# Moving GpSimd's part of a decoder layer's middle stage to VectorE and ScalarE

## The chip, the cores and the metric

One core of a Trainium2 chip runs the whole kernel. The metric is the time of one execution on the device in microseconds; lower is better. Engines are named as in the profile: PE (matrix products, PEld its weight loads), DVE (VectorE), ACT (ScalarE), POOL (GpSimd), SP (which issues most transfers). Each engine carries out its own queue strictly in order; the order of every queue is fixed when the kernel is built, by a scheduler that plans with its own idea of durations.

## The reference

One layer for 256 new prompt tokens and 8 decoded tokens (264 columns, T), width 2048, all in fp32: a half-step SwiGLU FFN of width 5504, a mixing stage, a second FFN, a final norm. In the mixing stage half the width is windowed attention, the other half is RWKV-7 time mixing. What the change touches is the time mixing:

```python
prev = jnp.concatenate([shift0[:, None].astype(proj.dtype), proj[:, :-1]], axis=1)
xm = (proj + mu * (prev - proj)).astype(f32)          # token shift
...
a = jax.nn.sigmoid(a0.astype(f32) + al @ a2.astype(f32))
kk = k * k_k.astype(f32)
k = k * (1.0 + (a - 1.0) * k_a.astype(f32))
...
kk = kk / jnp.maximum(jnp.sqrt(jnp.sum(kk * kk, axis=-1, keepdims=True)), 1e-12)
...
def step(S, inp):
    r_t, lw_t, k_t, v_t, kk_t, a_t = inp
    sa = jnp.einsum('bhij,bhj->bhi', S, -kk_t)
    S = (S * jnp.exp(lw_t)[:, :, None, :] + sa[..., None] * (kk_t * a_t)[:, :, None, :]
         + v_t[..., None] * k_t[:, :, None, :])
    return S, jnp.einsum('bhij,bhj->bhi', S, r_t)
```

## The kernel before

**Activations** lie transposed: 128 features on the partitions, 264 tokens along the free dimension. A **weight block** of 128 x 512 goes through `chunk` (lines 115 to 124): SP loads it into `raw` (ring of 6), ACT casts it to `hi` (ring of 4, line 122), and `lo = raw - hi` is made by DVE or, in the mixing stage for the third of a tile's four blocks (`LOP = (8,)`, argument `pool`), by POOL. Three products of 128 x 128 by 264 columns per 128 rows (hi by hi, hi by lo, lo by hi) give fp32 accuracy; a full tile is 16 x 3 = 48 products into one of three PSUM tiles `acc`.

**The stages.** First FFN, mixing, second FFN. In the FFNs PE works on such tiles only. In **mixing** 38 tiles of the input projection come in the order of `SEQ`: two tiles for the decay and gate inputs (`la`, `sgl`), then for each of 8 head pairs p three tiles (receptance, key, value: `xrr`, `xk`, `xv`) in four batches of two pairs, then keys and values of attention (4), then queries (8). Then the output projection in three passes (`PASS`).

**Side work.** After every weight block `gemm` calls `tick`, which advances every open generator by one step, so that small work is laid between blocks; the scheduler then orders it further by priority.

- `shifted` (331 to 341): DVE evicts a tile times the norm's factor into `pj` (columns 1 to 264; column 0 is zeroed by POOL for each tile); POOL subtracts neighbours, for the 256 prompt columns and the 8 decode columns; DVE's `scalar_tensor_tensor` multiplies by mu and adds.
- `prep` (351 to 451), one per pair: decay and gate factors, normalised key `kk`, products `b = kk*a` and `rk`, the factors `W`, `Wi`; then the key blocks. `KR` holds -kk and r times their decay, `BK` holds b and kx divided by decay, per chunk c of 64 tokens two slots of 64 columns: the head on partitions 0 to 63 has b in slot 0 and kx in slot 1, the other head the reverse, so that four half-height POOL products fill it. Line 420 multiplies both slots by `KR`; lines 443 to 450 transpose `BK` on PE and copy it to `t`.
- `chain` (463 to 612), one per batch, after both preps: triangular systems by 30 scan steps on DVE (tiles `X`, `Xt`, `st`), to and from DRAM for the layout (`sa`, `sb`, `TT`), then a transposition (`TN`) and small products on PE, then the states and a group norm.
- `dec_rwkv`: the decode tokens' state update, 16 rounds of DVE and POOL products (`ld`, `XR`), once the last prep is done; `attend` and `dec_attend`: attention.

Temporaries come from a ring of `NT` = 27 tiles `t`, side PSUM from five tiles `m`.

Of the kernel before, what the change touches and what calls it, by code (L numbers as in the profile page):

```python
# [13 lines left out]
P = 128  # L14
# [12 lines left out]
BATCH = [2, 2, 2, 2]  # L27
CH, NRAW, NHL = 4, 6, 4
NACC, NM = 3, 5
NS, NH, NT, NLD = 53, 40, 27, 6  # L30
NGM, NKR, NUV, NTT = 10, 5, 3, 2
NSTEP = 4
DWAIT = (8, 8, 8, 4)
LOP = (8,)
PW = (2, 1, 3, 2, 2)
ALPHA = math.exp(-0.5)
LKV = 26
# [9 lines left out]
def body(tc, I, O):  # L47
# [46 lines left out]
    with ExitStack() as ctx:  # L94
# [28 lines left out]
                tt(e, lo[:, :w], raw[:, :w], hi[:, :w].bitcast(F32), ALU.subtract)  # L123
            return hi, lo

        def gemm(ps, src, xs, step=None, rng=None, pool=False, ahead=True):
            n = len(xs)
            for k0 in range(0, n, CH):
                k1 = min(n, k0 + CH)
                if rng and k0 not in rng:  # L130
                    continue
                hi, lo = chunk(src[:, k0 * P:k1 * P], k1 - k0, G if pool and k0 in LOP else V, ahead)
                for k in range(k0, k1):
                    xh, xl = xs[k]
                    c = slice((k - k0) * P, (k - k0 + 1) * P)
                    mm(ps[:, :T], hi[:, c], xh, k == 0, False)
                    mm(ps[:, :T], hi[:, c], xl, False, False)
                    mm(ps[:, :T], lo[:, c], xh, False, k == n - 1)
                if step:
                    step()  # L140
# [149 lines left out]
        def mixing_body(mx, n2, n3):  # L290
# [18 lines left out]
            tw = fix((65, T), "tw")  # L309
            G.memset(tw[64:65, :], 1.0)  # L310
            rs = fix((P, T), "rs")
            qd = fix((P, 2, NB, 4), "qd")
            XR = fix((P, 6, 64), "XR")
            yr = fix((P, 64), "yr")
# [7 lines left out]

            def win(t):
                ps = acc()
                gemm(ps, I["win"][t], n2.xs, tick, pool=True)
                if not have[0]:
                    n2.rstd(rs)
                    have[0] = True
                return ps

            def shifted(t, d):
                ps = win(t)
                pj = ring((P, 268), "pj", 3)
                G.memset(pj[:, 0:1], 0.0)
                with tc.high_priority():
                    tt(V, pj[:, 1:1 + T], ps[:, :T], rs, ALU.mult)
                G.tensor_copy(shc[:, t, :], pj[:, NP:NP + NB + 1])
                tt(G, d[:, :NP], pj[:, 0:NP], pj[:, 1:NP + 1], ALU.subtract)
                tt(G, d[:, NP:], ss[:, t, :], pj[:, NP + 1:NP + 1 + NB], ALU.subtract)
                stt(d, d, vc(VMU + t), pj[:, 1:1 + T], ALU.mult, ALU.add)  # L340
                return d

            la, sgl = fix((P, T), "la"), fix((P, T), "sgl")
# [7 lines left out]
            def prep(p, bt, k, xrr, xk, xv):  # L351
                lw = load(I["lw"][p], (P, 256))
                zp = mp()
                for tb in range(2):
                    mm(zp[:, tb * P:(tb + 1) * P], tw[0:65, tb * P:(tb + 1) * P], lw[0:65, 0:P])
                mm(zp[:, 256:264], lw[0:65, 0:P], tw[0:65, NP:T])
                ap = mp()
                mm(ap[:, :T], lw[64:128, P:2 * P], la[64:128, :])
                sg, a = tmp(), tmp()
                act(sg, zp[:, :T], AF.Sigmoid)  # L360
                act(a, ap[:, :T], AF.Sigmoid, bias=vc(VA0 + p))
                kk, sq = tmp(), tmp()
                act(kk, xk, AF.Copy, scale=vc(VKK + p))
                act(sq, kk, AF.Square)
                bor = tmp((P, P))
                ts(G, bor, bo, vc(VRK + p), ALU.mult)
                yield from pause(PW[0])
                nps = mp()
                mm(nps[:, :T], bo, sq)
                cps = mp()  # L370
                for tb in range(2):
                    mm(cps[:, tb * P:(tb + 1) * P], sg[:, tb * P:(tb + 1) * P], tri)
                nr = tmp()
                act(nr, nps[:, :T], AF.Sqrt)
                V.reciprocal(nr, nr)
                cv = cps[:, :NP].rearrange("p (c t) -> p c t", c=4)
                W, Wi = tmp((P, 4, 65)), tmp((P, 4, 64))
                G.memset(W[:, :, 0:1], 1.0)
                act(W[:, :, 1:65], cv, AF.Exp, scale=-ALPHA)
                act(Wi, cv, AF.Exp, scale=ALPHA)  # L380
                tc.keep_in_program_order(act(XD[:, 1, p, :], sg[:, NP:T], AF.Exp, scale=-ALPHA))
                G.tensor_copy(wc[:, p, :], W[:, :, 64])
                yield from pause(PW[1])
                b, kx, rk = tmp(), tmp(), tmp()
                stt(kk, nr, 1e12, kk, ALU.min, ALU.mult)
                tt(G, b, kk, a, ALU.mult)
                ts(V, a, a, 1.0, ALU.subtract, vc(VKA + p), ALU.mult)
                stt(kx, a, 1.0, xk, ALU.add, ALU.mult)
                tt(G, rk, xrr, kx, ALU.mult)
                yield  # L390
                BK, KR = ring((P, 4, 2, 64), "bk", 2), ring((P, 3, 4, 64), "kr", NKR)
                bt.KR[k] = KR
                stt(KR[:, 0], c4(kk), -1.0, W[:, :, 0:64], ALU.mult, ALU.mult)
                tt(G, KR[:, 1], c4(xrr), W[:, :, 1:65], ALU.mult)
                for h in range(2):
                    r = HALF[h]
                    tt(G, BK[r, :, h, :], c4(b)[r], Wi[r], ALU.mult)
                    tt(G, BK[r, :, 1 - h, :], c4(kx)[r], Wi[r], ALU.mult)
                for i, src in ((0, kk), (2, b), (3, xv), (4, kx), (5, xrr)):
                    G.tensor_copy(XD[:, i, p, :], src[:, NP:T])  # L400
                vp = mp()
                for tb in range(2):
                    TE.transpose(vp[:, tb * P:(tb + 1) * P], xv[:, tb * P:(tb + 1) * P], ident)
                for e in range(2):
                    for h in range(2):
                        A.copy(bt.UV[HALF[1 - h], e:4:2, k, HALF[h]],
                               vp[HALF[e], :256].rearrange("p (c t) -> p c t", c=2)[:, :, HALF[h]])
                yield from pause(PW[2])
                bps = mp()
                mm(bps[:, :T], bor, rk)  # L410
                bv = tmp()
                bt.bv[k] = bv
                tt(V, bv, bps[:, :T], xv, ALU.mult)
                G.tensor_copy(bvdec[:, p, :], bv[:, NP:T])
                yield
                for h in range(2):
                    r = HALF[h]
                    gp = mp()
                    for c in range(4):
                        mm(gp[:, c * P:(c + 1) * P], BK[r, c, :, :], KR[r, 0:2, c, :])  # L420
                    gm = ring((P, 4, P), "gm", NGM)
                    bt.Gm[k][h] = gm
                    tt(V, gm, gp.rearrange("p (c t) -> p c t", c=4), bc(msk.unsqueeze(1), (P, 4, P)), ALU.mult)
                    for blk in range(2):
                        x = blk * 32
                        SP.dma_start(
                            scr[bt.i].rearrange("(h b k c) (s t) -> h b k s c t", h=2, b=2, c=4, s=32)[h, blk, k],
                            gm[h * 64 + x:h * 64 + x + 32, :, x:x + 32])
                    yield
                kp = mp()  # L430
                for tb in range(2):
                    TE.transpose(kp[:, tb * P:(tb + 1) * P], KR[:, 0, 2 * tb:2 * tb + 2, :], ident)
                for e in range(2):
                    for h in range(2):
                        A.copy(KR[HALF[h], 0, e:4:2, :],
                               kp[HALF[e], :256].rearrange("p (c t) -> p c t", c=2)[:, :, HALF[h]])
                gv = mp()
                for h in range(2):
                    r, o = HALF[h], HALF[1 - h]
                    for c in range(4):  # L440
                        mm(gv[r, c * 64:c * 64 + 64], bt.Gm[k][h][o, c, 0:64], bt.UV[o, c, k, r])
                A.copy(KR[:, 2], gv[:, :256].rearrange("p (c t) -> p c t", c=4))
                for tb in range(2):
                    bp = mp()
                    for j in range(2):
                        TE.transpose(bp[:, j * P:(j + 1) * P], BK[:, 2 * tb + j, :, :], ident)
                    t = tmp((P, 2, P))
                    A.copy(t, bp[:, :256].rearrange("p (c t) -> p c t", c=2))
                    bt.BT[k].append(t)
                    yield  # L450
                bt.left -= 1
# [560 lines left out]
```

## Time and profile before

| | us |
|---|---|
| median of 3 runs | 2128.84 (2128.02 to 2131.24) |
| the profiled execution | 2127.34 |
| its span, first to last instruction | 2125.2 |
| first input-projection tile evicted | 778.2 |
| last input-projection tile evicted | 1207.4 |
| first output-projection tile evicted | 1250.1 |
| last output-projection tile evicted | 1357.2 |

The profile is one execution. "Busy" is the time in which an engine had an instruction under way; the ends of PE's products are modelled, so PE's busy share also counts slow stretches. Rows of instruction groups read: line, engine, operation, output tile and inputs, shape, count, busy time and mean duration, and the idle time before them with the engine that ended it. The granted clock is the share of PE's full clock.

### The profile page before, as it was taken

How to read it: one execution, taken by the hardware profiler on the slowest of the kernel's cores; microseconds unless marked ns; L12 is line 12 of the kernel's file. 1: busy time of each engine (PE TensorE's matmuls, PEld its weight loads, DVE VectorE, ACT ScalarE, POOL GpSimd, SP SyncE). 2: the span in 40 equal slices, each digit the busy share in tenths (PEclk: the TensorE clock that was granted, in tenths of full speed). 3: DMA queues.
4: the chain of work that ended last, by engine and by line, in shares of the span. 5: the costliest groups of instructions: out<-in, count | busy, mean ns of one | idle time of the engine just before them, and what ended most of it. 6: DMA issues, size and time to landing. Idle time of an engine off the chain costs nothing.

```text
span 2125.2 us, 45168 instructions
## 1 busy us (share of the span) xinstructions
PE 2043.9 (96%) x16870; PEld 1995.4 (94%) x16870; DVE 1334.3 (63%) x2551; ACT 1045.8 (49%) x2002; POOL 419.5 (20%) x581
## 2 busy tenths in 40 slices
PE   8999999999999999989996899999999999999997
PEld 8999999999999999888885679899999999999997
DVE  5765555556555677766888646755555565555555
ACT  5644444444444566546542344644444444444445
POOL 0301011010201146533454201220110102011012
PEclk9999999999999999989997579999999999999999
DMA  6565565656555574434343145456555565555554
GB/s 224 176 182 182 175 205 175 207 180 183 181 177 185 185 227 139 122 96 135 112 136 114 41 138 186 156 182 181 181 175 187 177 184 181 177 186 176 186 176 140
DMA packets 227532, 356.27 MB, mean 168 GB/s; under 512 B 42176, under 2 KB 83152, under 8 KB 227280
## 3 DMA queue, kind: packets, MB, share of 16 engines
q1 hardware_dynamic: 221616, 344.72, 51.8%
q10 hardware_dynamic: 5696, 8.66, 1.1%
q8 instruction: 132, 2.16, 0.4%
q14 instruction: 88, 0.72, 0.1%
HBM read 345.15 MB, written 10.21 MB: 167 GB/s over the span
## 4 chain that ended last, share of the span: by engine, by line
PE 86%; DVE 7%; DMA 2%; ACT 1%; issue 1%; POOL 1%; SPq 1%; DVEq 0%; POOLq 0%; ACTq 0%
PE acc L73 79%; PE m L73 6%; DVE lo L57 1%; DMA raw<-in_gu 1%; DVE Xt L57 1%; DVE st L57 1%; ACT L67 1%; DVE ld L57 0%; ACT t L67 0%; DMA sb<-Xt 0%; DVE s L60 0%; DVE t L57 0%; DMA TT<-sb 0%; DVE TT L57 0%; DVE t L64 0%
## 5 line engine op out<-in xcount | busy, mean ns | idle before, releaser
L73 PE MATMUL acc<-s,hi 128*128 128x264 f32 x7072 | 1317.5, 286 | 10.0 <-ACT hi L122 8.3
L57 DVE TENSOR_TENSOR lo<-raw,hi 128x512 fp32r<-128x512 f32 (+1 forms) x1266 | 861.7, 684 | 600.6 <-ACT hi L122 578.7
L122 ACT CAST hi<-raw 128x512 fp32r<-128x512 f32 (+2 forms) x1304 | 780.5, 602 | 909.5 <-PE acc L73 830.6
L73 PEld LDWEIGHTS acc<-s,hi 128*128 128x128 f32 x7072 | 1108.8, 190 | 17.8 <-ACT hi L122 8.5
L73 PE MATMUL acc<-s,lo 128*128 128x264 f32 x3536 | 1016.1, 288 | 12.7 <-DVE lo L57 10.5
L73 PEld LDWEIGHTS acc<-s,lo 128*128 128x128 f32 x3536 | 669.9, 189 | 18.5 <-DVE lo L57 14.1
L73 PE MATMUL acc<-t,hi 128*128 128x264 f32 x2752 | 502.7, 284 | 1.6 <-ACT t L251 1.6
L73 PEld LDWEIGHTS acc<-t,hi 128*128 128x128 f32 x2752 | 426.0, 188 | 1.9 <-ACT t L251 1.8
L57 POOL TENSOR_TENSOR t<-t,t 128x264 f32<-128x264 f32 (+1 forms) x162 | 173.0, 1068 | 1209.6 <-ACT hi L122 897.6
L73 PE MATMUL acc<-t,lo 128*128 128x264 f32 x1376 | 388.2, 284 | 0.0
L73 PEld LDWEIGHTS acc<-t,lo 128*128 128x128 f32 x1376 | 258.2, 188 | 0.0
L57 DVE TENSOR_TENSOR t<-acc,t 128x264 f32<-128x264 f32 x164 | 70.9, 433 | 36.7 <-PE acc L73 36.5
L57 POOL TENSOR_TENSOR s<-s,s 128x264 f32<-128x264 f32 (+1 forms) x56 | 49.5, 886 | 195.8 <-ACT s L67 179.1
L57 POOL TENSOR_TENSOR lo<-raw,hi 128x512 fp32r<-128x512 f32 x38 | 49.7, 1308 | 57.4 <-ACT hi L122 57.2
L67 ACT ACT_TABLE_LOAD x42 | 53.9, 1283 | 1.9 <-PEq L1004 1.2
L60 DVE SCALAR_TENSOR_TENSOR s<-acc,s 128x264 f32<-128x264 f32 x96 | 40.7, 428 | 16.8 <-PE acc L73 16.3
L60 DVE SCALAR_TENSOR_TENSOR x<-acc,x 128x264 f32<-128x264 f32 x96 | 40.6, 427 | 10.9 <-PE acc L73 10.4
L57 DVE TENSOR_TENSOR st<-X,Xt 128x60 f32<-128x60 f32 (+10 forms) x120 | 36.1, 300 | 10.1 <-DMA Xt<-sa 7.4
L67 ACT ACTIVATE t<-t 128x264 f32<-128x264 f32 x94 | 40.0, 425 | 3.3 <-DVE t L57 1.8
L57 DVE TENSOR_TENSOR Xt<-Xt,st 128x60 f32<-128x60 f32 (+10 forms) x120 | 36.7, 305 | 1.7
L251 ACT CAST t<-t 128x264 fp32r<-128x264 f32 x86 | 35.5, 413 | 3.6 <-POOL t L57 2.1
L73 PE MATMUL m<-s,hi 128*128 128x264 f32 x160 | 30.1, 287 | 0.4 <-ACT hi L122 0.4
(209 smaller groups left out, 1116.5 us busy)
## 6 DMA issues: line engine op xcount, KB each, us to landing
raw<-in_gu SPq DMA_DIRECT2D x688, 256.0 KB, 3.2
raw<-in_dn SPq DMA_DIRECT2D x224, 256.0 KB, 2.7
raw<-in_win SPq DMA_DIRECT2D x152, 256.0 KB, 3.2
raw<-in_dn SPq DMA_DIRECT2D x160, 192.0 KB, 2.7
raw<-in_wout SPq DMA_DIRECT2D x48, 256.0 KB, 3.0
raw<-in_wout SPq DMA_DIRECT2D x32, 128.0 KB, 2.4
xsp<-x ACTq DMA_DIRECT2D x16, 132.0 KB, 3.5
s<-xsp SPq DMA_DIRECT2D x16, 132.0 KB, 3.0
```

Of the source, the lines that this page charges most:

```text
L57: return e.tensor_tensor(out=out, in0=a, in1=b, op=op)
L60: return V.scalar_tensor_tensor(out=out, in0=a, scalar=s, in1=b, op0=op0, op1=op1)
L67: return A.activation(out=out, in_=in_, func=f, **k)
L73: TE.matmul(out, lhsT, rhs, start=start, stop=stop, **k)
L122: A.copy(hi[:, :w], raw[:, :w])
L251: A.copy(hi, u)
```

## The change

Six edits, all in the mixing stage:

1. All four splits of a projection tile are DVE's (`LOP` and `pool` go).
2. Token shift: three fixed `pj` tiles, whose column 0 is zeroed once. `nmu` = 1 - mu and mu times the shift states are made once. Per tile ACT writes mu times the shifted columns into `d` and copies the 8 state columns; DVE's `scalar_tensor_tensor` adds (1 - mu) times `pj`.
3. `b`, `rk` and the second block of `KR` are DVE's, `bor` is ACT's.
4. `BK` has three slots per chunk: b in slots 0 and 2, kx in slot 1, written by one wide and one narrow DVE product on all partitions. A head reads slots h and h+1.
5. With three slots the transposition is done per head and chunk as a product with a 64 x 64 identity, eight per pair into two `m` tiles, and four copies put the halves together.
6. `NT` goes from 27 to 25.

The lines of the changed program are a few higher or lower than those of the program before.

```diff
--- before.py
+++ after.py
@@ -27,11 +27,10 @@
 BATCH = [2, 2, 2, 2]
 CH, NRAW, NHL = 4, 6, 4
 NACC, NM = 3, 5
-NS, NH, NT, NLD = 53, 40, 27, 6
+NS, NH, NT, NLD = 53, 40, 25, 6
 NGM, NKR, NUV, NTT = 10, 5, 3, 2
 NSTEP = 4
 DWAIT = (8, 8, 8, 4)
-LOP = (8,)
 PW = (2, 1, 3, 2, 2)
 ALPHA = math.exp(-0.5)
 LKV = 26
@@ -123,13 +122,13 @@
                 tt(e, lo[:, :w], raw[:, :w], hi[:, :w].bitcast(F32), ALU.subtract)
             return hi, lo
 
-        def gemm(ps, src, xs, step=None, rng=None, pool=False, ahead=True):
+        def gemm(ps, src, xs, step=None, rng=None, ahead=True):
             n = len(xs)
             for k0 in range(0, n, CH):
                 k1 = min(n, k0 + CH)
                 if rng and k0 not in rng:
                     continue
-                hi, lo = chunk(src[:, k0 * P:k1 * P], k1 - k0, G if pool and k0 in LOP else V, ahead)
+                hi, lo = chunk(src[:, k0 * P:k1 * P], k1 - k0, V, ahead)
                 for k in range(k0, k1):
                     xh, xl = xs[k]
                     c = slice((k - k0) * P, (k - k0 + 1) * P)
@@ -309,6 +308,13 @@
             tw = fix((65, T), "tw")
             G.memset(tw[64:65, :], 1.0)
             rs = fix((P, T), "rs")
+            PJ = [fix((P, 268), f"pj{i}") for i in range(3)]
+            for pj in PJ:
+                G.memset(pj[:, 0:1], 0.0)
+            nmu = fix((P, NSH), "nmu")
+            mu = vec[:, VMU:VMU + NSH]
+            ts(V, nmu, mu, -1.0, ALU.mult, 1.0, ALU.add)
+            tt(V, ss, ss, bc(mu.unsqueeze(2), (P, NSH, NB)), ALU.mult)
             qd = fix((P, 2, NB, 4), "qd")
             XR = fix((P, 6, 64), "XR")
             yr = fix((P, 64), "yr")
@@ -322,7 +328,7 @@
 
             def win(t):
                 ps = acc()
-                gemm(ps, I["win"][t], n2.xs, tick, pool=True)
+                gemm(ps, I["win"][t], n2.xs, tick)
                 if not have[0]:
                     n2.rstd(rs)
                     have[0] = True
@@ -330,14 +336,13 @@
 
             def shifted(t, d):
                 ps = win(t)
-                pj = ring((P, 268), "pj", 3)
-                G.memset(pj[:, 0:1], 0.0)
+                pj = PJ[t % 3]
                 with tc.high_priority():
                     tt(V, pj[:, 1:1 + T], ps[:, :T], rs, ALU.mult)
                 G.tensor_copy(shc[:, t, :], pj[:, NP:NP + NB + 1])
-                tt(G, d[:, :NP], pj[:, 0:NP], pj[:, 1:NP + 1], ALU.subtract)
-                tt(G, d[:, NP:], ss[:, t, :], pj[:, NP + 1:NP + 1 + NB], ALU.subtract)
-                stt(d, d, vc(VMU + t), pj[:, 1:1 + T], ALU.mult, ALU.add)
+                act(d[:, :NP], pj[:, 0:NP], AF.Copy, scale=vc(VMU + t))
+                A.copy(d[:, NP:], ss[:, t, :])
+                stt(d, pj[:, 1:1 + T], nmu[:, t:t + 1], d, ALU.mult, ALU.add)
                 return d
 
             la, sgl = fix((P, T), "la"), fix((P, T), "sgl")
@@ -363,7 +368,7 @@
                 act(kk, xk, AF.Copy, scale=vc(VKK + p))
                 act(sq, kk, AF.Square)
                 bor = tmp((P, P))
-                ts(G, bor, bo, vc(VRK + p), ALU.mult)
+                act(bor, bo, AF.Copy, scale=vc(VRK + p))
                 yield from pause(PW[0])
                 nps = mp()
                 mm(nps[:, :T], bo, sq)
@@ -383,19 +388,18 @@
                 yield from pause(PW[1])
                 b, kx, rk = tmp(), tmp(), tmp()
                 stt(kk, nr, 1e12, kk, ALU.min, ALU.mult)
-                tt(G, b, kk, a, ALU.mult)
+                tt(V, b, kk, a, ALU.mult)
                 ts(V, a, a, 1.0, ALU.subtract, vc(VKA + p), ALU.mult)
                 stt(kx, a, 1.0, xk, ALU.add, ALU.mult)
-                tt(G, rk, xrr, kx, ALU.mult)
-                yield
-                BK, KR = ring((P, 4, 2, 64), "bk", 2), ring((P, 3, 4, 64), "kr", NKR)
+                tt(V, rk, xrr, kx, ALU.mult)
+                yield
+                BK, KR = ring((P, 4, 3, 64), "bk", 2), ring((P, 3, 4, 64), "kr", NKR)
                 bt.KR[k] = KR
                 stt(KR[:, 0], c4(kk), -1.0, W[:, :, 0:64], ALU.mult, ALU.mult)
-                tt(G, KR[:, 1], c4(xrr), W[:, :, 1:65], ALU.mult)
-                for h in range(2):
-                    r = HALF[h]
-                    tt(G, BK[r, :, h, :], c4(b)[r], Wi[r], ALU.mult)
-                    tt(G, BK[r, :, 1 - h, :], c4(kx)[r], Wi[r], ALU.mult)
+                tt(V, KR[:, 1], c4(xrr), W[:, :, 1:65], ALU.mult)
+                s4 = (P, 4, 2, 64)
+                tt(V, BK[:, :, 0:3:2, :], bc(c4(b).unsqueeze(2), s4), bc(Wi.unsqueeze(2), s4), ALU.mult)
+                tt(V, BK[:, :, 1, :], c4(kx), Wi, ALU.mult)
                 for i, src in ((0, kk), (2, b), (3, xv), (4, kx), (5, xrr)):
                     G.tensor_copy(XD[:, i, p, :], src[:, NP:T])
                 vp = mp()
@@ -417,7 +421,7 @@
                     r = HALF[h]
                     gp = mp()
                     for c in range(4):
-                        mm(gp[:, c * P:(c + 1) * P], BK[r, c, :, :], KR[r, 0:2, c, :])
+                        mm(gp[:, c * P:(c + 1) * P], BK[r, c, h:h + 2, :], KR[r, 0:2, c, :])
                     gm = ring((P, 4, P), "gm", NGM)
                     bt.Gm[k][h] = gm
                     tt(V, gm, gp.rearrange("p (c t) -> p c t", c=4), bc(msk.unsqueeze(1), (P, 4, P)), ALU.mult)
@@ -440,12 +444,15 @@
                     for c in range(4):
                         mm(gv[r, c * 64:c * 64 + 64], bt.Gm[k][h][o, c, 0:64], bt.UV[o, c, k, r])
                 A.copy(KR[:, 2], gv[:, :256].rearrange("p (c t) -> p c t", c=4))
+                bps = [mp(), mp()]
+                for c in range(4):
+                    for h in range(2):
+                        r = HALF[h]
+                        mm(bps[h][:, c * 64:c * 64 + 64], BK[r, c, h:h + 2, :], ident[r, r])
                 for tb in range(2):
-                    bp = mp()
-                    for j in range(2):
-                        TE.transpose(bp[:, j * P:(j + 1) * P], BK[:, 2 * tb + j, :, :], ident)
                     t = tmp((P, 2, P))
-                    A.copy(t, bp[:, :256].rearrange("p (c t) -> p c t", c=2))
+                    for h in range(2):
+                        A.copy(t[:, :, HALF[h]], bps[h][:, tb * P:tb * P + P].rearrange("p (c t) -> p c t", c=2))
                     bt.BT[k].append(t)
                     yield
                 bt.left -= 1
```

## The prediction

> **What bounds the kernel now.** I read the page's busy rows first, then busy time by stage, then the waits inside the stage that the change touches.
>
> ```profile
> PE 2043.9 (96%) x16870; PEld 1995.4 (94%) x16870; DVE 1334.3 (63%) x2551; ACT 1045.8 (49%) x2002; POOL 419.5 (20%) x581
> PEclk9999999999999999989997579999999999999999
> ```
> ```profile
> 1500.00:1550.00 50.00, 50.00 (x414) 50.00 (x413) 27.32 (x43) 24.16 (x42) 8.62 (x8) 1.00 0.52 181
> ...
> 778.00:859.00 81.00, 80.66 (x658) 78.04 (x657) 50.59 (x73) 53.08 (x101) 49.33 (x90) 1.00 0.51 153
> 859.00:1081.00 222.00, 203.13 (x1911) 188.79 (x1912) 172.50 (x405) 114.40 (x245) 100.93 (x182) 0.94 0.43 119
> 1081.00:1207.00 126.00, 98.27 (x821) 84.92 (x816) 102.02 (x293) 41.29 (x109) 51.61 (x68) 0.78 0.33 96
> 1207.00:1250.00 43.00, 35.57 (x140) 23.66 (x140) 23.45 (x93) 20.63 (x69) 4.60 (x14) 0.58 0.26 75
> ```
> The columns of the second view are length, PE, PEld, DVE, ACT and POOL busy, then granted clock and DMA. In the FFN (1500 to 1550) PE issues 414 matmuls in 50 us, 0.121 us each, at full clock: weights set the time there and nothing of the change can help. A projection tile is 48 such matmuls, 5.8 us; 38 tiles would be 220 us, but from the first eviction (778) to the last (1207) pass 429 us. From 778 to 859 PE is full and DVE has 30 us to spare. From 859 to 1207 DVE works 274.5 of 348 us (79%) and no engine is full: DVE's queue carries the weight splits, the scans and the preparation in one order, PE waits for pieces of it, and the clock drops to 0.94 and 0.78. From 1207 to 1250 no tile is left and the end of batch 3 and attention run as a chain at clock 0.58.
>
> ```profile
> PE m L73 <- DVE TN L506: 12.4, 1, 12.4
> ```
> This is PE's longest wait, from its waits between 1130 and 1180: in PE's order the triangular products of batch 3 stand behind all 38 tiles, and they need its scan, which DVE ends at 1151 (the scan's rows below). So what DVE has to do up to there passes to the end, unless idle time on DVE takes it up.
>
> **What GpSimd does here, and what it does to DVE.** GpSimd's rows for 778 to 1207; the first five leave it (with a few small ones), the last three stay:
>
> ```profile
> L57 POOL TENSOR_TENSOR lo<-raw,hi 128x512 fp32r<-128x512 f32 x36 | 47.1, 1308 | 56.0 <-ACT hi L122 55.9
> L57 POOL TENSOR_TENSOR bk<-t,t 64x256 f32<-64x256 f32 x32 | 27.3, 853 | 1.2
> L57 POOL TENSOR_TENSOR t<-pj 128x256 f32<-128x256 f32 x24 | 18.7, 781 | 0.0
> L57 POOL TENSOR_TENSOR t<-t,t 128x264 f32<-128x264 f32 x16 | 15.9, 997 | 12.6 <-DVE t L60 11.5 <-ACT uv L406 1.1
> L57 POOL TENSOR_TENSOR kr<-t,t 128x256 f32<-128x256 f32 x8 | 6.0, 745 | 0.0
> ...
> L57 POOL TENSOR_TENSOR t<-ld,XR 128x256 f32<-128x256 f32 x32 | 26.0, 818 | 4.7 <-ACT XR L636 3.4 <-DMA ld<-in_st 0.7
> L57 POOL TENSOR_TENSOR ld<-ld,t 128x256 f32<-128x256 f32 x16 | 12.5, 781 | 32.2 <-PE m L73 18.5 <-DVE ld L57 8.4 <-DVE st L57 2.3
> L57 POOL TENSOR_TENSOR t<-XR 128x256 f32<-128x256 f32 x16 | 11.8, 736 | 24.3 <-DVE sa L649 24.3
> ```
> The first five are 115.0 us, the last three 50.3. Now DVE's rows. The first fence has the splits of the mixing stage, then those of an FFN stretch (1400 to 1750), where GpSimd hardly works; the second the scan's two groups with their means, then the same groups' minimum, median and maximum; the third eviction and token shift.
>
> ```profile
> L57 DVE TENSOR_TENSOR lo<-raw,hi 128x512 fp32r<-128x512 f32 x110 | 86.8, 794 | 17.4 <-ACT hi L122 16.6
> L57 DVE TENSOR_TENSOR lo<-raw,hi 128x512 fp32r<-128x512 f32 x216 | 149.6, 692 | 129.6 <-ACT hi L122 123.3 <-PE acc L73 1.9
> L57 DVE TENSOR_TENSOR t<-t,t 128x264 f32<-128x264 f32 x3 | 1.3, 429 | 0.0
> L57 DVE TENSOR_TENSOR gm<-m,C 128x512 f32<-128x512 f32 x16 | 10.6, 680 | 1.2 <-PE m L73 1.1
> ```
> ```profile
> L57 DVE TENSOR_TENSOR st<-X,Xt 128x60 f32<-128x60 f32 (+10 forms) x120 | 36.1, 300 | 10.1 <-DMA Xt<-sa 7.4
> L57 DVE TENSOR_TENSOR Xt<-Xt,st 128x60 f32<-128x60 f32 (+10 forms) x120 | 36.7, 305 | 1.7
> ...
> L57 DVE TENSOR_TENSOR st<-X,Xt x120: 121/216/1285, 858.6 to 1151.2; 128x60 f32<-128x60 f32 x16, 128x28 f32<-128x28 f32 x8, 128x48 f32<-128x48 f32 x8, 128x42 f32<-128x42 f32 x8
> L57 DVE TENSOR_TENSOR Xt<-Xt,st x120: 130/214/1271, 858.9 to 1151.4; 128x60 f32<-128x60 f32 x16, 128x28 f32<-128x28 f32 x8, 128x48 f32<-128x48 f32 x8, 128x42 f32<-128x42 f32 x8
> ```
> ```profile
> L57 DVE TENSOR_TENSOR pj<-acc,rs x26: 371/426/437, 778.2 to 1023.7; 128x264 f32<-128x264 f32 x26
> L60 DVE SCALAR_TENSOR_TENSOR t<-t,vec,pj x24: 479/493/1633, 788.5 to 1044.3; 128x264 f32<-128x264 f32 x24
> ...
> L60 DVE SCALAR_TENSOR_TENSOR t<-t,vec,pj 128x264 f32<-128x264 f32 x24 | 15.3, 638 | 8.4 <-POOL t L57 8.4
> ```
> Operations with one operand from PSUM (pj) never exceed 437 ns; those with two operands from SBUF reach 1.3 to 1.6 us where their median is 0.2 to 0.5. The excess over the undisturbed value: splits 110 x (794 - 692) = 11.2 us, scan 120 x (300 - 216 + 305 - 214) = 21.0, shift 24 x (638 - 493) = 3.5; 35.7 us in all (the scan's part is an estimate, its shapes differ).
>
> The Trainium skill, SBUF — State Buffer, section Who interferes with whom, says that a DVE instruction with two SBUF inputs and a GpSimd instruction that reads SBUF share one read interface, and that the second to issue waits for the whole of the first. By that rule the excess leaves with GpSimd's instructions and the sum below stands; were the cause another, nothing would come back. The split of the rows into PSUM and SBUF operands agrees.
>
> **The change part by part.**
>
> *Added to DVE.* The nearest rows for products of 256 columns are the decode's; they show too when its GpSimd part begins:
>
> ```profile
> L57 POOL TENSOR_TENSOR t<-ld,XR x32: 719/736/1170, 1071.9 to 1201.8; 128x256 f32<-128x256 f32 x32
> L57 DVE TENSOR_TENSOR ld<-ld,XR x16: 407/416/884, 1073.0 to 1196.2; 128x256 f32<-128x256 f32 x16
> ```
> 38 splits x 0.692 = 26.3. Products b and rk, 16 x 0.429 = 6.9. The second KR block and the narrow key block, 16 x 0.416 = 6.7. The wide key block, 8 of 512 columns at 0.680: 5.4. Sum 45.3. The shift's last operation keeps its 493 ns. Scaling the shift states and 1-mu are two operations in FFN 1, where DVE is about half idle. Of the 45.3, 12 splits (8.3) and two pairs' preparation (2 x 2.4) fall before 859 and vanish in DVE's 30 idle us there. 32 us land in the stretch where DVE counts.
>
> *Taken off DVE.* At most the 35.7; at least the part by GpSimd's share of time, 115.0 of 165.3 (70%), less a quarter before 859: 19. I take 27, nearer the middle, because the operations that stay begin at 1072. Net on DVE: +5 (bounds -4 and +13).
>
> *Waits.* The 8.4 us for which DVE waited for GpSimd's subtractions end. Instead it waits for ACT.
>
> ```profile
> L67 ACT ACTIVATE t<-t,vec 128x264 f32<-128x264 f32 x8 | 4.1, 514 | 0.0
> L67 ACT ACTIVATE XD<-t 128x8 f32<-128x8 f32 x8 | 1.7, 212 | 0.0
> ```
> A scaled copy and the state's copy are 0.51 + 0.21 = 0.72 us, against 0.78 and 0.22 on GpSimd. In ACT's new queue each scaled copy mostly stands behind the same cast whose split DVE has ahead of the shift, so it meets no further block; behind it stand the next casts, later by 0.72 us, with a ring of four. I take 4 us of new waits (0 to 8.4): -4. PE's waits for GpSimd's splits add -2:
>
> ```profile
> PE acc L73 <- POOL lo L57: 1.9, 2, 1.5
> ```
> *Preparation as a chain.* From the chain of waits:
>
> ```profile
> 807.87 0.65 POOL kr L57
> ...
> 809.65 1.13 POOL t L57
> 811.11 1.16 POOL bk L57
> 812.34 0.73 POOL bk L57
> 813.41 1.25 POOL lo L57
> 814.66 2.35 POOL t L57 x3
> 817.01 0.70 POOL bk L57
> 817.78 0.81 POOL bk L57
> ```
> Eight pieces, 8.8 us, set the pace around the first pair. On DVE the same steps of a pair are 2.4 us, but behind its splits. I take half of 8.8 back, -4 (bounds 0 and -8.8), since PE is nearly full there.
>
> *The rest.* The key blocks' transposition becomes eight half-height products and four small copies for four and two, and bor moves to ACT (about 0.4 us a pair): ACT is busy 208.8 of 429 us from 778 to 1207 and PE waits elsewhere, so I charge +1 (bounds 0 and 5; without that cover 8 x 0.6). Two temporaries fewer: 0 while the ring has free slots, a rival below.
>
> Sum: +5 - 4 - 2 - 4 + 1 = -4, rounded up in size to -5, because a stretch without long PE waits also keeps its clock. The profiled execution took 2127.34 (span 2125.2 and 2.1 around it), 1.5 below the median 2128.84. Forecast: 2122.
>
> **The rivals.**
>
> *DVE becomes the bound (slower).* 32 us more in one queue; only 13 come back, because the products now on DVE also push the scans back: in the new order of DVE's queue the scans start two or three tiles later for batch 3, amid more splits. It decides if batch 3's scan ends later than about 1151. Then the net 19 us pass to the end one to one, since PE has no tiles left: 2146. For it: 102.0 of 126 us busy from 1081 and the 12.4 us wait. Against it: DVE still has 73 idle us from 859 to 1207. Should none of the excess return: 32 less 5, 2154.
>
> *The stalls collapse (much faster).* All 35.7 return (net -4), the waits go without replacement (-10), the chain gives its 8.8, and the 13 us that clock 0.94 costs of 222 halve: -29, 2098. For it: the largest excesses sit in the scans, ahead of which PE stalls. Against it: PE's own tile order is hardly changed, and batch 3 still comes after all tiles.
>
> *No change.* GpSimd's and DVE's shares cancel and the waits only change their releaser: DVE's order now waits for ACT, a 25-slot ring holds preparation back by as much as the chain gains. 2127. For it: 32 against 27. Against it: the chain rows name GpSimd.
>
> **How the numbers follow.** Forecast (own range 2112 to 2125) 0.37, DVE as bound 0.30, no change 0.18, collapse 0.15. Within 0.2%, about what a measurement of this kernel can tell from no change, is 2124.6 to 2133.1. Faster: 0.15 and most of 0.37, 0.47; same: most of 0.18 and the forecast's upper edge, 0.20; slower 0.33. The range takes in the collapse's lesser half and the DVE rival's 2146: 2100 to 2147.
>
> **What would show it.** Right: splits at 692 ns and scan means near 216 throughout to 1070; DVE busy from 778 to the last tile about 5 us more; GpSimd at least 115 us less over the span, no wait of DVE or PE for it before 1070; the wait for TN no longer than 12.4. Wrong: the shift's operation waiting more than 8 us for ACT, the scans' records still long, a longer TN wait, or clock below 0.94 in the middle.

## The result, and the profile after

| | before | after |
|---|---|---|
| median (4 runs each on this chip) | 2128.43 us | 2112.80 us (2108.01 to 2115.03) |
| ratio | | 0.9922, 95% interval 0.9909 to 0.9935 |
| profiled execution | 2127.34 us | 2113.38 us |
| its span | 2125.2 us | 2111.5 us |
| end of batch 3's scan | 1151 | 1136 |
| first, last output tile evicted | 1250.1, 1357.2 | 1236.7, 1343.4 |

The kernel is 0.8% faster: 14.0 us between the profiled executions, 16 us between the medians. The direction is the forecast's, the size about three times its 5 us. By the end of batch 3's scan the gain is complete (15 us); from there on both kernels take the same time.

Busy time by stage of the changed kernel (length, PE, PEld, DVE, ACT, POOL busy, granted clock, DMA):

```profile
778.00:859.00 81.00, 81.00 (x681) 78.43 (x680) 53.69 (x104) 59.02 (x127) 13.72 (x31) 1.00 0.54 161
859.00:1081.00 222.00, 218.00 (x2193) 204.04 (x2193) 177.03 (x475) 129.68 (x303) 44.96 (x82) 0.98 0.47 129
1081.00:1207.00 126.00, 92.27 (x652) 75.72 (x650) 98.08 (x306) 43.69 (x122) 38.67 (x54) 0.70 0.27 79
1207.00:1250.00 43.00, 41.32 (x225) 31.59 (x224) 19.55 (x70) 17.11 (x54) 4.39 (x13) 0.66 0.43 121
```
PE issues 2193 products in 859 to 1081 where it issued 1911, and the clock there is 0.98 instead of 0.94. What is left for 1081 to 1207 is less, and it runs at a lower clock (0.70).

The same view of each kernel from the first eviction to the end of batch 3's scan, before first:

```profile
778.00:1151.00 373.00, 340.75 (x3061) 318.21 (x3059) 292.42 (x668) 193.78 (x407) 188.12 (x320) 0.95 0.45 128
```
```profile
778.00:1136.00 358.00, 340.14 (x3163) 319.04 (x3161) 285.10 (x742) 209.51 (x481) 83.40 (x145) 0.96 0.47 134
```
DVE carries out 74 instructions more and is busy 7.3 us less; its idle time falls from 80.6 to 72.9 us. Together that is the 15 us by which the stretch is shorter. For PE the same rows say: 102 products more in the same busy time (340.8 and 340.1 us), and 17.9 us idle instead of 32.3. How DVE could take on the added instructions shows in its groups (the changed kernel, 778 to 1207; then the scan's means over the kernel and its minimum, median and maximum):

```profile
L56 DVE TENSOR_TENSOR lo<-raw,hi 128x512 fp32r<-128x512 f32 x146 | 101.8, 703 | 26.4 <-ACT hi L121 24.6 <-PE m L72 0.6 <-DMA sa<-gm 0.2
...
L59 DVE SCALAR_TENSOR_TENSOR t<-pj,nmu,t 128x264 f32<-128x264 f32 x24 | 11.7, 490 | 7.7 <-ACT t L344 7.7
...
L56 DVE TENSOR_TENSOR st<-X,Xt 128x60 f32<-128x60 f32 (+10 forms) x120 | 28.1, 234 | 12.9 <-DMA Xt<-sa 6.6 <-DMA ld<-in_g 4.8
L56 DVE TENSOR_TENSOR Xt<-Xt,st 128x60 f32<-128x60 f32 (+10 forms) x120 | 26.4, 220 | 1.7
```
```profile
L56 DVE TENSOR_TENSOR st<-X,Xt x120: 140/209/722, 854.6 to 1135.1; 128x60 f32<-128x60 f32 x16, 128x28 f32<-128x28 f32 x8, 128x48 f32<-128x48 f32 x8, 128x42 f32<-128x42 f32 x8
L56 DVE TENSOR_TENSOR Xt<-Xt,st x120: 147/207/766, 854.8 to 1136.0; 128x60 f32<-128x60 f32 x16, 128x28 f32<-128x28 f32 x8, 128x48 f32<-128x48 f32 x8, 128x42 f32<-128x42 f32 x8
```
The split went from 794 to 703 ns, the scan's two groups from 300 and 305 to 234 and 220, the shift's last operation from 638 to 490; no operation of the scan takes 1.3 us any more. PE's waits from 780 to 1060, before and after:

```profile
PE acc L73 <- DVE lo L57: 6.2, 4, 3.1
PE m L73 <- DVE gm L57: 5.3, 4, 3.1
PE m L73 <- DVE Xt L57: 2.8, 1, 2.8
PE m L73 <- DVE st L57: 2.1, 1, 2.1
```
```profile
PE m L72 <- DVE TN L513: 1.0, 1, 1.0
PE acc L72 <- DVE lo L56: 0.5, 2, 0.3
```
With the 1.9 us for GpSimd's splits these were 18.3 us; 1.5 are left.

### The profile page after: what moved, and what is told of

Same layout as the page of the kernel before. It is cut to its first block, busy times and chain, and to the rows that moved or that the text cites. A ratio compares the mean times of both kernels' runs of the same rounds, so it can differ in the third digit from the quotient of the medians.

```text
span 2111.5 us, 45349 instructions
## 1 busy us (share of the span) xinstructions
PE 2045.6 (97%) x16966; PEld 1997.4 (95%) x16966; DVE 1327.7 (63%) x2631; ACT 1061.5 (50%) x2078; POOL 311.1 (15%) x404
## 4 chain that ended last, share of the span: by engine, by line
PE 92%; DVE 4%; DMA 1%; ACT 1%; issue 1%; SPq 0%; DVEq 0%; ACTq 0%
PE acc L72 83%; PE m L72 9%; DVE lo L56 1%; DMA sb<-Xt 0%; DVE ld L56 0%; DMA raw<-in_gu 0%; DVE t L56 0%; DVE st L56 0%; ACT L66 0%; DVE y L56 0%; DVE t L631 0%; DVE s L59 0%; ACT t L66 0%; PE m L737 0%; DVE Xt L56 0%
## 5 line engine op out<-in xcount | busy, mean ns | idle before, releaser
L56 DVE TENSOR_TENSOR lo<-raw,hi 128x512 fp32r<-128x512 f32 (+2 forms) x1304 | 876.6, 676 | 606.4 <-ACT hi L121 583.2
L56 POOL TENSOR_TENSOR t<-t,t 128x264 f32<-128x264 f32 (+1 forms) x146 | 156.8, 1074 | 1197.3 <-ACT hi L121 897.5
L56 DVE TENSOR_TENSOR t<-acc,t 128x264 f32<-128x264 f32 x164 | 70.9, 432 | 36.9 <-PE acc L72 36.5
L59 DVE SCALAR_TENSOR_TENSOR s<-acc,s 128x264 f32<-128x264 f32 x96 | 40.6, 427 | 16.6 <-PE acc L72 16.1
L56 DVE TENSOR_TENSOR st<-X,Xt 128x60 f32<-128x60 f32 (+10 forms) x120 | 28.1, 234 | 12.9 <-DMA Xt<-sa 6.6
L342 POOL COPY shc<-pj 128x9 f32<-128x9 f32 x26 | 20.0, 768 | 85.9 <-DVE pj L56 85.9
L66 ACT ACTIVATE t<-t,sta 128x256 f32<-128x256 f32 (+2 forms) x33 | 14.7, 446 | 28.3 <-DVE sta L63 27.1
```

The source lines that it names most:

```text
L56: return e.tensor_tensor(out=out, in0=a, in1=b, op=op)
L59: return V.scalar_tensor_tensor(out=out, in0=a, scalar=s, in1=b, op0=op0, op1=op1)
L66: return A.activation(out=out, in_=in_, func=f, **k)
```

## The experiments

All changes are given as ratios to the kernel before on the same chip, with 95% intervals; us are the ratio's distance from 1 times 2128.

| kernel | ratio | interval | us | scan ends |
|---|---|---|---|---|
| changed kernel | 0.9922 | 0.9909 to 0.9935 | -17 | 1136 |
| e1_splits (edit 1) | 0.9921 | 0.9905 to 0.9937 | -17 | 1139 |
| e2_shift (edit 2) | 0.9966 | 0.9952 to 0.9979 | -7 | 1148 |
| e3_blocks (edits 3 to 6) | 0.9939 | 0.9924 to 0.9955 | -13 | 1147 |
| e4_no_splits (edits 2 to 6) | 0.9952 | 0.9932 to 0.9973 | -10 | 1145 |
| e9_splits_shift (edits 1, 2) | 0.9956 | 0.9940 to 0.9973 | -9 | 1144 |
| e8_no_shift (edits 1, 3 to 6) | 0.9948 | 0.9933 to 0.9963 | -11 | 1139 |
| e10_other_plan | 0.9939 | 0.9924 to 0.9955 | -13 | 1138 |
| e5_idle_read | 1.0016 | 1.0004 to 1.0029 | +3 | 1162 |
| e6_idle_write | 0.9971 | 0.9959 to 0.9984 | -6 | 1140 |
| e7_cast_wait | 0.9980 | 0.9970 to 0.9991 | -4 | 1148 |
| e11_scan_steps | 0.9927 | 0.9906 to 0.9948 | -16 | 1124 |
| e12_decode_dve | 0.9967 | 0.9955 to 0.9979 | -7 | 1139 |

**The parts of the change.** The first alone is one argument:

```diff
-                hi, lo = chunk(src[:, k0 * P:k1 * P], k1 - k0, G if pool and k0 in LOP else V, ahead)
+                hi, lo = chunk(src[:, k0 * P:k1 * P], k1 - k0, V, ahead)
```


> Edit 1 alone: all weight splits of the projection on DVE, the rest as before. Blocking theory (the gain is what GpSimd's two-operand instructions kept DVE from doing): 38 splits leave GpSimd, which give DVE back about 18 us of stretched instructions and load it with 26 us, 8 of them before 859 where DVE is idle: 0 us, time near 2127. Queue theory (the preparation of the pairs stood behind splits on GpSimd that themselves waited 49 us for ACT's casts): most of the gain comes here, 10 us, time near 2117.

The other two take the change's lines for the shift, or for the products, key blocks, transposition and ring, into the kernel before; the fourth puts the old third split back into the changed kernel.

> Edit 2 alone: token shift as a scaled copy on ACT and one DVE operation (26 temporaries, for room). Blocking theory: 2 to 4 us of stretch and 8 us of DVE's waits for GpSimd go, 4 to 8 us of waits for ACT come: 2 to 6 us faster, near 2123. Queue theory: GpSimd's queue is 25 us shorter, but the splits with their waits stay in it: 3 us, near 2124.

> Edits 3 to 6 alone: products and three-slot key blocks on DVE, transposition by eight products, 25 temporaries. Blocking theory: 18 us of stretch go, 19 us of DVE work come, 5 of them where DVE is idle: 4 us faster, near 2123, the scan's means near 240 ns. Queue theory: the preparation no longer stands behind splits on GpSimd, so that as much is gained as in edit 1: 10 us, near 2117.

> Edits 2 to 6, with the third split of a projection tile on GpSimd as before. Blocking theory: as the changed kernel within 3 us (18 us of stretch return, 18 us of DVE work in the part that counts go). Queue theory: also as the changed kernel, since nothing of the preparation is left in GpSimd's queue; but DVE has 26 us less to do, so it may be up to 8 us faster than the changed kernel, 2105.

Edit 1 alone gives all of the gain, where the blocking theory, as it was priced, gave 0. Edits 3 to 6 alone give most of it too, the shift some. In e1 and e3 the queue theory's 10 us come nearer than the blocking theory's 0 and 4. Without edit 1 the others stay at -10, 6 us behind the changed kernel, where both theories had e4 within 3 us of it or ahead. Added up, the three would be -37. So they largely take away the same thing, and edit 1 is the one that the changed kernel needs.

Where edit 1's gain lies shows in its row from 778 to the end of its scan, to be read against the row of before up to 1151:

```profile
778.00:1139.00 361.00, 331.78 (x3059) 310.63 (x3058) 291.44 (x705) 192.66 (x407) 150.29 (x284) 0.97 0.48 132
```
PE has issued as many products (3059, before 3061) in 12 us less: it is busy for 9.0 us less, at clock 0.97 instead of 0.95, and idle for 3.0 us less. From 900 to 950 the clock is 0.83 before and 0.97 in e1. DVE is busy as long as before (291.4 and 292.4 us), so a net of about 0 on DVE's time, as the blocking theory had it, was right here, and the gain came all the same. DVE's idle time falls by 11.0 us; its wait for PE's tiles ahead of the evictions falls by 16.8, while others grow (before first):

```profile
DVE pj L57 <- PE acc L73: 19.7, 9, 5.9
```
```profile
DVE pj L57 <- PE acc L73: 2.9, 3, 2.5
```
What raised the clock no run here isolates.

Whether any one edit adds to it can't be told here: with edit 1 the shift costs 7 us (e9), with the key blocks as well it brings 6 (e8 against the changed kernel).

```diff
-                pj = PJ[t % 3]
+                pj = ring((P, 268), "pj", 3)
+                G.memset(pj[:, 0:1], 0.0)
...
+                tt(G, d[:, :NP], pj[:, 0:NP], pj[:, 1:NP + 1], ALU.subtract)
```


> The changed kernel with the old token shift (edits 1 and 3 to 6). Blocking theory: GpSimd's 25 us of two-operand subtractions return, 2 to 4 us of stretch, ACT has 18 us less: within 4 us of the changed kernel, 2109 to 2117. Were the parts additive as e2_shift measured it (7 us), it would be 2120.

> Edits 1 and 2 (26 temporaries). If the three parts remove the same stalls, so that the first of them takes the whole gain: within 4 us of e1_splits, 2110 to 2117. If the shift's gain of 7 us measured alone adds up: 2106.

e9_splits_shift lies half a us above what one common stall allows and far from what adding up gave; e8_no_shift lies between the two, and doesn't tell them apart. What speaks against adding up is the sum of -37 above, and that e9 brings 7 us less than edit 1 alone instead of 7 more.

**What GpSimd's split did.** Three kernels put something into GpSimd's queue in place of each of the 38 splits, with the splits themselves on DVE:

```diff
+                if pool and k0 in LOP:
+                    extra(hi, lo)
...
+        # e5_idle_read
+            tt(G, s, C[:, 0:512], C[:, 128:640], ALU.subtract)
+        # e6_idle_write
+            G.memset(s, 0.0); G.memset(s, 0.0); G.memset(s[:, :256], 0.0)
+        # e7_cast_wait
+            G.tensor_copy(s[:, 0:1], hi[:, 0:1].bitcast(F32))
```


> The splits on DVE as in e1_splits, but GpSimd gets in the place of each of its 38 splits a subtraction of two fixed tiles of 128 x 512 into a scratch tile, which waits for nothing and which nobody waits for (25 temporaries, for room). Blocking theory: GpSimd reads two SBUF operands for 50 us more, DVE's two-operand instructions are stretched again by about 18 us, and with 26 us more on DVE the time is at least that of the kernel before, 2124 to 2138. Occupancy theory (only the preparation behind it in GpSimd's queue is late): 2117 to 2122, as in the run with writes. Theory that the wait for ACT's cast in GpSimd's queue did it: 2113 as e1_splits.

> As e5_idle_read, with three memsets of the scratch tile (1280 columns together, about 1.3 us) in place of the subtraction: GpSimd is as long occupied but reads nothing. Blocking theory (it is the read side that is shared): DVE is not stretched, only GpSimd's queue is longer: 2113 to 2118. Occupancy theory: as e5_idle_read within 3 us.

> As e5_idle_read, with a copy of one column of the block's cast in place of the subtraction: GpSimd's queue again waits at each of 38 places for ACT's cast, but for hardly any work. Theory that this wait held up the pairs' preparation: 2121 to 2128. Blocking and occupancy theories: 2113 to 2116. It also shows what another order of the queues from the planner is worth, since the work of DVE and PE is that of e1_splits.

In e5 and e6 the idle instructions, which wait for nothing, run early (34 of the 38 between 778 and 859) and fill GpSimd there. That makes the cleanest comparison; the stage's row of e1_splits, e5_idle_read and e6_idle_write:

```profile
778.00:859.00 81.00, 79.71 (x651) 76.99 (x650) 51.00 (x80) 54.77 (x106) 36.45 (x82) 1.00 0.55 158
```
```profile
778.00:859.00 81.00, 71.94 (x543) 67.62 (x542) 70.32 (x71) 42.86 (x81) 77.01 (x96) 0.97 0.48 135
```
```profile
778.00:859.00 81.00, 80.42 (x657) 77.74 (x656) 52.85 (x82) 53.40 (x102) 74.45 (x184) 1.00 0.56 156
```
GpSimd is equally full in both (77.0 and 74.5 us). Where it reads two operands, DVE is busy 70.3 us for 71 instructions instead of 51.0 for 80, and PE issues 108 products fewer, 13 us of them at 0.121. Where it writes only, DVE's busy time and PE's products hardly change. In time the two kernels are about 10 us apart. PE's longest waits from 778 to 859 in e5 are for splits (e1 lists no wait there):

```profile
PE acc L73 <- DVE lo L57: 8.3, 7, 2.9
```
The splits' rows in 778 to 1207 say the same of DVE, 851 ns (e5) and 741 ns (e6) against 732 in e1_splits:

```profile
L57 DVE TENSOR_TENSOR lo<-raw,hi 128x512 fp32r<-128x512 f32 x146 | 123.0, 851 | 18.5 <-ACT hi L122 18.1 <-PE acc L73 0.2
```
```profile
L57 DVE TENSOR_TENSOR lo<-raw,hi 128x512 fp32r<-128x512 f32 x146 | 107.1, 741 | 20.8 <-ACT hi L122 19.1 <-ACT t L459 0.6
```
The Trainium skill, SBUF — State Buffer, section Who interferes with whom, makes just this distinction: a DVE instruction with two SBUF inputs contends with a GpSimd instruction that reads SBUF, not with one that only writes. The runs agree.

But e6 does not stay where the blocking theory put it (-14 to -9): -6, with DVE's waits for GpSimd's subtractions at 12.1 us instead of 6.3. And e7, where GpSimd copies one column, is at -4, 13 us behind e1; its copies wait 68 us for ACT's casts:

```profile
L130 POOL COPY scratch<-hi 128x1 f32<-128x1 f32 x36 | 14.3, 398 | 68.3 <-ACT hi L122 68.2
```
So a queue in which the pairs' preparation stands behind something that is long, or waits, seems to have a price of its own. By which path e7's 13 us reach the end is not shown: the listed waits for GpSimd grow little (DVE's for the subtractions from 6.3 to 7.8 us, and 4.1 us for ACT). Blocking alone does not explain e7, and a late queue alone does not explain e5 against e6.

The planner sets another order for each of these kernels. What that alone can do:

> e1_splits with 21 temporaries: the same instructions, but the planner sets another order over about half of the mixing stage (25 or 22 temporaries would leave every queue as it is). Theory that GpSimd's reads, occupancy and waits cost the time: 2111 to 2118, as e1_splits. Theory that the differences seen so far are those of one planned order against another: it may lie anywhere between 2105 and 2128, and a value above 2120 would leave e6_idle_write and e7_cast_wait open.

It is at -13, inside the expectation and within 4 us of e1_splits. Differences of some 4 us between single kernels are therefore not read here. Even that may be too little: e9 is 7 us behind e1 although it takes work off GpSimd, and its shift waits only 1.5 us for ACT. e5 against e1 (20 us) and e7 against e1 (13 us) stand above both, e6 against e10 (7 us) does not.

**What sets the end now.** In the changed kernel:

```diff
-                    if s % NSTEP == 0:
+                    if s % (NSTEP if bt.i < 3 else 10) == 0:
```


> The changed kernel with batch 3's scan given out in portions of ten steps instead of four, so that it stands earlier in DVE's queue. If the end of batch 3's scan sets the end one to one: the scan ends 5 to 10 us earlier and so does the kernel, 2103 to 2108. If the attention behind the last tiles sets it as well: 2110 to 2116.

The scan's last operation starts 12 us earlier, the end hardly moves:

```profile
L56 DVE TENSOR_TENSOR Xt<-Xt,st x120: 146/206/725, 854.4 to 1124.2; 128x60 f32<-128x60 f32 x16, 128x28 f32<-128x28 f32 x8, 128x48 f32<-128x48 f32 x8, 128x42 f32<-128x42 f32 x8
```
PE's longest wait there, from 780 to 1207:

```profile
PE m L72 <- DVE TN L513: 18.7, 2, 17.7
```
PE's wait for batch 3 is longer (18.7 instead of 11.8 us from 780 to 1207), and the last output tile comes at 1339.1 instead of 1343.4. The scan's end alone does not pass through one to one; the ratio can't be told from the changed kernel's.

```diff
-                    tt(G, t1, S, bj(0), ALU.mult)
+                    tt(V, t1, S, bj(0), ALU.mult)
...
-                    tt(G, t2, S, bj(5), ALU.mult)
+                    tt(V, t2, S, bj(5), ALU.mult)
```


> The changed kernel with the decode's 64 products of 128 x 256 on DVE too, so that GpSimd has almost nothing left from 1072 on. Blocking theory: the remaining stretch of about 16 us before the scan's end goes and with it DVE's 3.4 us wait for GpSimd, against 64 x 0.416 = 27 us more on DVE, where it is 78% busy and sets the end: 5 to 10 us slower than the changed kernel, 2118 to 2123. Were GpSimd's slowness the cost and not DVE's time: 2105 to 2110.

```profile
L56 DVE TENSOR_TENSOR st<-X,Xt x120: 138/209/251, 854.3 to 1139.1; 128x60 f32<-128x60 f32 x16, 128x28 f32<-128x28 f32 x8, 128x48 f32<-128x48 f32 x8, 128x42 f32<-128x42 f32 x8
```
With GpSimd out of the way the scan's longest operation takes 251 ns: the remaining stretch of the changed kernel (up to 722) was the decode's. Yet the kernel is 10 us slower than the changed one, as expected: what comes back is less than the 27 us more on DVE. Up to the end of its scan the durations of DVE's instructions add up to 339.7 us, in the changed kernel to 329.9. The profiled execution shows 4.3 of the 10 us: the scan ends 3.3 us later, the last output tile comes at 1348.0 instead of 1343.4. No kernel here beats the changed one beyond its interval.

## Why the prediction was right, and where its size was wrong

**The mechanism.** That GpSimd's reads stretch DVE's operations with two SBUF operands, and that the excess leaves with them, is shown: by the rows after, by e5 against e6, and by e12's 251 ns. That this carried the whole gain is not shown. Edit 1 alone gains as much with DVE busy as long as before, and e7, which reads a single column 38 times, loses 13 of edit 1's 17 us. The prediction had GpSimd's queue in its sum only as half of an 8.8 us chain and 2 us of PE's waits, and the clock only as the rounding from -4 to -5; in e1 PE takes 9.0 us less for the same number of products. The direction came out as argued. That the time still falls 0.8 us inside the forecast's own range (2112 to 2125) with its terms off by this much is partly luck.

**The term that was mis-sized** is "Net on DVE: +5 (bounds -4 and +13)". Measured by busy time up to the end of the scan it is -7.3, outside its bounds. Two things were missing. The excess returned is larger than the 27 us taken: 110 splits x (794 - 703 ns) = 10.0 us, the scan's two groups 120 x (66 + 85) = 18.1, shift 24 x (638 - 490) = 3.6, and three groups that the prediction left out, the pairs' other two-operand operations, the scan's blocks after their way through DRAM, and the first `KR` block:

```profile
L60 DVE SCALAR_TENSOR_TENSOR t<-t,t 128x264 f32<-128x264 f32 x16 | 9.7, 607 | 0.1
L57 DVE TENSOR_TENSOR TT<-TT,C 32x256 f32<-32x256 f32 x16 | 9.3, 582 | 12.1 <-DMA TT<-sb 11.8
L60 DVE SCALAR_TENSOR_TENSOR kr<-t,t 128x256 f32<-128x256 f32 x8 | 7.7, 964 | 0.1
```
```profile
L59 DVE SCALAR_TENSOR_TENSOR t<-t,t 128x264 f32<-128x264 f32 x16 | 6.8, 424 | 0.0
L56 DVE TENSOR_TENSOR TT<-TT,C 32x256 f32<-32x256 f32 x16 | 6.7, 416 | 10.8 <-DMA TT<-sb 10.4
L59 DVE SCALAR_TENSOR_TENSOR kr<-t,t 128x256 f32<-128x256 f32 x8 | 3.3, 418 | 0.0
```
They give 2.9, 2.7 and 4.4 more, 41.7 in all. The durations of all of DVE's instructions up to the scan's end add up to nearly the same in both kernels, 329.3 us for 668 and 329.9 us for 742: what was added came back, and no more. And busy time is a union of records, in which a record mostly begins a little before the one ahead ends. The overlap is 329.3 - 292.4 = 36.9 us before and 329.9 - 285.1 = 44.8 us after; the 7.3 us are this overlap and not less work.

**Waits.** DVE's waits for the shift did not fall by 4 us: 8.4 for GpSimd became 7.7 for ACT. What fell was PE's: 18.3 to 1.5 us until 1060, of which the sum had only GpSimd's own 1.9 and the chain's 4. DVE's idle time is 7.7 us lower: over the stretch from 780 to 1207 its wait for PE's tiles ahead of the evictions falls from 19.7 to 7.1 us, that for ACT's casts grows from 16.6 to 24.6.

**The cover before 859** held for this change: PE issues 681 products there instead of 658. It is no rule that DVE's idle time there hides everything. In e5 PE does 13 us less in that very stretch and waits 8.3 us for splits, although DVE is idle for 10.7 of 81 us.

**The signs that the prediction named.** Until 1070 DVE and PE have no wait for GpSimd, the wait for `TN` is 10.8 us, the shift's operation waits 7.7 us for ACT, and the clock in the middle is 0.98, all as a right prediction asked. Two did not come: DVE's busy time up to the last projection tile is 4.3 us less and not 5 more (321.2 and 325.5), and GpSimd's falls by 108.4 us (419.5 to 311.1) and not by 115, not least because its copy of 9 columns takes 20.0 us in all instead of 9.5 (last section).

**The rivals.** "DVE becomes the bound" did not come; a price of that kind is seen in e12 (10 us for 27 us more). "The stalls collapse" described what happened to the scans and the waits, but its 29 us assumed that chain and clock gains add up; half of it came. Its condition, that a stage without long waits keeps its clock, holds until 1081 (0.94 to 0.98) and is lost behind it (0.78 to 0.70).

**Still open:** why single edits don't add up beyond what another planned order explains, what raised the clock, and why e6 loses its time behind the scan, which ends as in e1_splits: its first output tile is evicted at 1240.3 instead of 1234.5, and from 1236 to 1270 its clock is 0.87 instead of 0.95.

## What to carry to other kernels

Before giving GpSimd elementwise work beside a busy VectorE, compare the minimum, median and maximum of VectorE's operations with two SBUF operands: the excess is part of the price of GpSimd instructions that read. Price a move by what VectorE gets back as well as by what it gets to do, group by group, and stop where the return is smaller (here at the decode's products). Look too at what stands behind an instruction that waits for another engine in a shared in-order queue: here 38 short copies with such waits came with 13 us. And test a compound change edit by edit; here one argument gave the whole gain.

## What was not expected of the hardware

Records of GpSimd grew as well: GpSimd's copy of 9 columns took 194 ns (median) before and takes 694, at most 3022, in the changed kernel, beside a VectorE that now runs more operations with two SBUF operands. No engine is listed as waiting for it. That DVE's reads are the cause is not shown: e8_no_shift has as many DVE instructions from 778 to 1024 (480, the changed kernel 477) and a median of 288 ns (at most 3049).

```profile
L337 POOL COPY shc<-pj x26: 185/194/730, 778.7 to 1024.1; 128x9 f32<-128x9 f32 x26
```
```profile
L342 POOL COPY shc<-pj x26: 191/694/3022, 779.7 to 990.5; 128x9 f32<-128x9 f32 x26
```
